# The tables of a state space layer: factors transposed once and read back, instead of a table transposed block by block

## The chip, the cores and the metric

The kernel runs on one core of a Trainium2 chip, as one launch. Its metric is device time in microseconds, the median of three runs. A profile of one further execution gives the busy time of each engine: TensorE (PE), VectorE (DVE), ScalarE (ACT), GpSimd (POOL) and SyncE (SP), which issues nearly all DMAs. All arithmetic is in float32; products on TensorE are made of exact parts (a value is split into a high part, `whi`, and a low part, `wlo`, and three products are added up).

## The reference

Two blocks follow each other on 256 tokens of 1024 features. The first has two layers, each with a mixer (pooling and a gated recurrence, then band attention), attention to a memory of 256 tokens, and an MLP with squared relu. The second has differential attention, an MLP, a state space layer and a last MLP. The state space layer is what the change is about:

```python
lam = lax.complex(a_re, a_im); dt = jnp.exp(log_dt)[..., None]
a_bar = jnp.exp(lam * dt)
b_bar = ((a_bar - 1.0) / lam)[..., None] * b_mat
def scan_dir(u_row, r, reverse):
    bu = jnp.einsum('sgh,gph->sgp', u_row.astype(jnp.complex64), b_bar[r])
    a = jnp.broadcast_to(a_bar[r], bu.shape)
    _, states = lax.associative_scan(_ssm_combine, (a, bu), reverse=reverse, axis=0)
    return jnp.einsum('sgp,ghp->sgh', states, c_mat[r]).real
```

There are 64 groups of 16 channels, each with 64 complex states in two directions. The kernel works through the scan in chunks of eight steps. For that it needs tables that depend on the weights alone: E, which carries eight inputs into the state at a chunk's end (powers of a times b), G, which reads eight outputs from the state at its start (powers of a times c), and the products of the two within a chunk.

## The kernel before, in words

The program is written layer by layer, and a scheduler orders the instructions of each engine by priority; each engine then runs its own list in order and waits on semaphores. Work that is marked `low` gets a lower priority, so that it falls between the instructions of the layer around it. DMAs on SP's queue are issued in order too, and a DMA that must wait for data holds up the ones behind it.

The four MLPs (`mlp`, line 275) have the same matmuls: for eight column chunks of 512, `ffps` is the product with the first weight, `relu` its squared relu, and `ffacc` adds up the product with the second. In the first two chunks the tokens are rows, and four `fftp` transposes turn each result (line 337); they come as matmuls with 512 columns. The other six chunks come as matmuls with 256. A weight tile of 512 KB is loaded (`raw`, line 42), its high part is made on ACT (lines 47 and 53) and its low part on DVE (lines 49 and 58).

An MLP can take a generator, `fill`, that it steps between its own products. The first MLP steps `ssm_scalars`: powers and phases of all 64 groups, on DVE, stored in `pk` and written to memory as `d_p`. The second MLP steps `ssm_tables` for blocks 0 to 7, the third for blocks 8 to 15 (a block has four groups); the fourth has no fill. The layer itself comes between the third and the fourth MLP and loads the tables again.

For a block, `ssm_tables` loads the coefficients (`bc`), the powers (`pk`) and the gain (`gb`). On DVE it makes `bb`, the input matrix, by a complex product. A complex product (`cmul`, line 1142) is four products and two combinations; with `second=G` two of its products run on GpSimd (lines 1149 and 1150). So come `er` and `gr`, with 512 columns for each real part. `gr` is written out as G. `er` has the states on the partitions and is turned by eight transposes into the `etp` tiles (line 1393); ACT copies them (`eo`, line 1394), and two DMAs write E (`d_e`). The klag matmuls (lines 1401 and 1405) make the products within a chunk from `bm` (copies of `bb`), the `c` part of `bc`, and `gr`.

Two pools matter on TensorE: `ps`, four PSUM banks that `ffps`, `fftp`, `etp` and `klag` share, and a second one of four banks for `ffacc`.

Of the kernel before, what the change touches and what calls it, by code (L numbers as in the profile page):

```python
# [24 lines left out]
class Seg:  # L25
    """A column block of a weight, its rows times a gain, split exactly into two float32r parts."""
# [42 lines left out]
class Core:  # L69
# [37 lines left out]
    def rstd(self, ms, n=1, scale=1.0, tag="r", bufs=None):  # L107
# [4 lines left out]
        if n >= 16:  # L112
            # a first guess from the exponent, then Newton's steps
# [19 lines left out]
    def feat_half(self, src, q, hi, lo, k0=None):  # L133
        """columns 512 q .. of src [128 tokens, 1024] -> hi, lo [128 features, 4 q .. (or k0 ..), 128 tokens]"""
# [15 lines left out]
    def row_scale_free(self, out):  # L150
        """the scales of the rows of X along the free axis: out [128, 256]"""
# [69 lines left out]
    def mm_b(self, out, wh, wl, xh, xl, first, last):  # L221
        """out [128 features, tokens] += w^T x"""
# [9 lines left out]
    def feat32(self, src, dst):  # L232
        """src [128 tokens, 1024] -> dst [128 features, 8, 128 tokens] in float32"""
# [8 lines left out]
    def proj_a(self, hh, hl, w, c0, done, gain=None, turns=((0, 0, 8), (1, 0, 8)), step=None, share=False, now=(0, 3)):  # L242
        """token-major [128, 1024] projections; the token tiles take turns: (tile, first and last step of the contraction)"""
# [15 lines left out]
    def proj_b(self, hh, hl, w, c0, consume, gain=None, groups=4):  # L259
        """feature-major projections of both token tiles: consume(g, [128 features, 2, 256]) for the columns 256 g .."""  # L260
# [14 lines left out]
    def mlp(self, pool, w1, gain, w2, done, perm=False, fill=None):  # L275
        """done(tt, acc, rsq): acc times rsq is the output; perm: tokens leave in the order (step in chunk, chunk)."""
# [116 lines left out]
class Halves:  # L393
    """activations [128, 2, 8, 128] in two tiles of four features each"""
# [9 lines left out]
class Attn:  # L404
    """attention sublayers; mixed into Core"""

    def mem_feat(self, parts, mem):
        """the memory over its root mean square, feature-major; kept for the other layer"""
# [23 lines left out]
    def two_parts(self, outs, src):  # L432
        """src as float32r parts"""
# [4 lines left out]
    def three(self, out, xs, ys, first, last):  # L438
        """out += x^T y, of float32r parts, or of float32 as it is"""
# [7 lines left out]
    def mem_keys(self, pool, parts, gain, w_kv, step=None):  # L447
        """feature-major: as float32r parts, or in float32 to take less room while there are steps to go along with"""
# [20 lines left out]
    def put_feat(self, ps, g, oh, ol):  # L469
        """ps [128 features, 2, 256 tokens] -> features 256 g .. as float32r parts"""  # L470
# [6 lines left out]
    def cross(self, pool, w_q, gain, kv, out, w_o, done):  # L477
        """out: the room for the heads' outputs, feature-major"""
# [56 lines left out]
    def band(self, pool, w_qkv, gain, relb, w_o, done):  # L535
        """relb: [16, 513]"""
# [10 lines left out]
        # the scales of the tokens along the free axis  # L547
# [8 lines left out]
        def scores(t, k0, nh):  # L556
            """heads of the features 128 k0 .. 128 (k0 + nh), queries of tile t"""
# [56 lines left out]
        def advance(g):  # L614
            """the scores of group g, the values of the group before"""
# [12 lines left out]
    def diff(self, pool, w_qkv, gain, q_gain, k_gain, lam_vecs, subln, w_o, cos2, sin2, done):  # L628
        """cos2, sin2: [256, 64], (cos | cos) and (-sin | sin)"""
# [32 lines left out]
        # the heads in two halves  # L662
# [11 lines left out]
        def part(c0, mid=None):  # L674
            """512 columns of both token tiles"""
# [12 lines left out]
        def prep(c, a, nm, dst):  # L688
            """rotated heads 8 c .. of both token tiles, feature-major; the root mean square is left to the scores for the queries"""
# [60 lines left out]
        def soft(t, g):  # L750
            """exponentials of the heads 4 g .. 4 g + 3; head 2 (2 g + i) + j is [j][i]"""
# [39 lines left out]
        def values(c):  # L791
            """the heads 4 c .. 4 c + 3, over their root mean square, into which the sums of the first softmax go"""
# [64 lines left out]
class Mixer:  # L857
    def even(self, pool, w_in, gain, pool_w, pool_scale, lb_logits, out_gain, w_out, masks, done, mem_feat, mem_keys):
        """pool_scale, lb_logits: [128, 4]; masks: [128, 5, 128]"""
# [90 lines left out]
        def queries(b, ps):  # L950
            """with the factor 1 - bound of the keys"""
# [6 lines left out]
        def pooling():  # L958
            """window sums by doubling, group g with the window 2 << g"""
# [19 lines left out]
        # decayed scores, transposed: [s, head, t] per token tile  # L979
# [27 lines left out]
        def levels():  # L1007
# [22 lines left out]
            # across the chunks of a tile, then across the tiles  # L1030
# [97 lines left out]
class Ssm:  # L1128
    """State space layer in chunks of L tokens. Groups are in the order (half, batch, q, strip) of group
    32 half + 8 strip + 4 batch + q; a block is four strips, a batch is four blocks."""  # L1130

    def ssm_scratch(self, dram):
# [3 lines left out]
        self.d_p = dram.tile([128, NG, 34], F32, name="d_p")  # L1136
# [5 lines left out]
    def cmul(self, pool, outr, outi, xr, xi, yr, yi, neg_i=False, tag="ct", second=None):  # L1142
        """(outr, outi) = x * y; with neg_i the imaginary part is negated"""
# [15 lines left out]
    def ssm_scalars(self, a_re, a_im, log_dt, sgn):  # L1159
# [700 lines left out]
```

## Time and profile before

| | |
|---|---|
| Median of three runs | 1508.09 us (1506.77 to 1510.31) |
| Span of the profiled execution | 1506.2 us |
| PE busy | 1426.7 us, 95% |
| DVE busy | 1138.3 us, 76% |
| ACT busy | 823.2 us, 55% |
| POOL busy | 203.4 us, 14% |
| DMA | 296.15 MB, mean 197 GB/s |

The profiled execution is known by its span, from the first to the last instruction; it lies 1.9 us below the median. The stages by time are: even mixer and memory attention to 231.8, first MLP to 416.0, band and memory attention to 641.1, second MLP to 863, differential attention to 989.2, third MLP to 1199.7, the state space layer to 1312, the last MLP to 1496. A busy share is a mean over these stages, and the limits differ between them, so a stage is read by itself: which engine is busy throughout, and what it waits for where it is not.

### The profile page before, as it was taken

To read this page: it belongs to the slowest core of one execution; us is meant where nothing else is said; L and a number is where in the kernel's file an instruction comes from. 1 tells how busy PE (TensorE), PEld (TensorE's weight loads), DVE (VectorE), ACT (ScalarE), POOL (GpSimd) and SP (SyncE) were. 2 spreads that over 40 slices of the span, in tenths; PEclk is the share of its full clock that TensorE was granted. 3 is DMA by queue.
4 is the path that set the end of the run, shared out by engine and by line. 5 is a ranking of instruction groups with operands and counts; after the bars stand their busy time and mean duration, and the time that the engine had idled before them with its cause. 6 is when DMAs were issued, how large, how long until landed. Compare 5 with 4: busy or idle time off the path is not lost.

```text
span 1506.2 us, 25237 instructions
## 1 busy us (share of the span) xinstructions
PE 1426.7 (95%) x9540; PEld 1239.2 (82%) x9540; DVE 1138.3 (76%) x2004; ACT 823.2 (55%) x1412; POOL 203.4 (14%) x219
## 2 busy tenths in 40 slices
PE   8899999999999999989899999999999877999997
PEld 8797888899889799869779877879789656889895
DVE  7986658988767775679994799889994688674651
ACT  7475546555564665655454777755453524664540
POOL 1241001000000000024430010124330131000000
PEclk9999999999999999999999999999999988999999
DMA  8455536465776355366667654256668956755640
GB/s 299 147 205 170 187 103 199 154 241 187 273 232 199 117 185 193 112 205 215 211 222 249 222 181 151 86 168 229 227 219 298 358 208 217 233 183 188 206 158 28
DMA packets 134034, 296.15 MB, mean 197 GB/s; under 512 B 16152, under 2 KB 36376, under 8 KB 133272
## 3 DMA queue, kind: packets, MB, share of 16 engines
q1 hardware_dynamic: 133624, 292.44, 57.8%
q0 software_dynamic: 288, 2.10, 0.4%
q8 instruction: 75, 1.23, 0.3%
q14 instruction: 47, 0.39, 0.1%
HBM read 269.10 MB, written 30.57 MB: 199 GB/s over the span
## 4 chain that ended last, share of the span: by engine, by line
PE 37%; DVE 15%; DMA 8%; issue 5%; ACT 2%; POOL 1%; SPq 0%; DVEq 0%; POOLq 0%; ACTq 0%
DVE wlo L58 4%; PE ffacc L218 4%; PE ffacc L219 4%; PE ffacc L217 4%; PE ffps L226 2%; PE ffps L224 2%; PE ffps L225 2%; DMA raw<-in_w_ff 2%; PE pacc L217 2%; PE pacc L218 2%; PE pacc L219 2%; DMA raw<-in_ffn_w_down 1%; DMA raw<-in_ffn_w_up 1%; PE pb L224 1%; PE pb L225 1%
## 5 line engine op out<-in xcount | busy, mean ns | idle before, releaser
L58 DVE SCALAR_TENSOR_TENSOR wlo<-raw,gcols,whi 128x512 fp32r<-128x512 f32 (+1 forms) x456 | 356.8, 825 | 68.8 <-ACT whi L53 68.5
L53 ACT ACTIVATE whi<-raw,gcols 128x512 fp32r<-128x512 f32 (+1 forms) x456 | 316.9, 745 | 126.5 <-DMA raw<-in_w_ff 26.9
L49 DVE TENSOR_TENSOR wlo<-raw,whi 128x1024 fp32r<-128x1024 f32 x172 | 207.1, 1221 | 64.9 <-ACT whi L47 64.4
L47 ACT ACTIVATE whi<-raw 128x1024 fp32r<-128x1024 f32 x176 | 182.1, 1055 | 91.7 <-DMA raw<-in_w_ff 28.3
L224 PE MATMUL ffps<-hh,whi 128*128 128x256 f32 x768 | 223.1, 290 | 0.0
L226 PE MATMUL ffps<-hl,whi 128*128 128x256 f32 x768 | 220.9, 288 | 0.0
L225 PE MATMUL ffps<-hh,wlo 128*128 128x256 f32 x768 | 220.5, 287 | 0.0
L217 PE MATMUL ffacc<-whi,ah 128*128 128x512 f32 x512 | 204.9, 401 | 0.0
L218 PE MATMUL ffacc<-wlo,ah 128*128 128x512 f32 x512 | 202.7, 396 | 0.1
L219 PE MATMUL ffacc<-whi,al 128*128 128x512 f32 x512 | 202.6, 396 | 0.0
L224 PEld LDWEIGHTS ffps<-hh,whi 128*128 128x128 f32 x768 | 149.3, 194 | 2.1 <-issue 1.6
L225 PEld LDWEIGHTS ffps<-hh,wlo 128*128 128x128 f32 x768 | 149.0, 194 | 0.5
L226 PEld LDWEIGHTS ffps<-hl,whi 128*128 128x128 f32 x768 | 148.8, 194 | 0.0
L219 PEld LDWEIGHTS ffacc<-whi,al 128*128 128x128 f32 x512 | 96.7, 189 | 22.9
L217 PEld LDWEIGHTS ffacc<-whi,ah 128*128 128x128 f32 x512 | 96.8, 189 | 22.5 <-issue 1.6
L218 PEld LDWEIGHTS ffacc<-wlo,ah 128*128 128x128 f32 x512 | 96.8, 189 | 21.5 <-DVE wlo L49 0.5
L225 PE MATMUL pb<-hh,wlo 128*128 128x256 f32 x352 | 100.5, 286 | 3.4 <-DVE wlo L58 3.4
L224 PE MATMUL pb<-hh,whi 128*128 128x256 f32 x352 | 100.1, 287 | 2.3 <-ACT whi L53 2.3
L226 PE MATMUL pb<-hl,whi 128*128 128x256 f32 x352 | 100.0, 285 | 0.0
L171 POOL TENSOR_TENSOR r<-r,mhalf 128x1 f32<-128x1 f32 x32 | 24.6, 768 | 535.0 <-DVE r L170 528.6
L299 DVE TENSOR_TENSOR relu<-relu 128x512 f32<-128x512 f32 x64 | 44.8, 701 | 59.1 <-ACT relu L298 58.9
L298 ACT ACTIVATE relu<-ffps 128x512 f32<-128x512 f32 x64 | 43.9, 686 | 76.9 <-PE ffps L226 62.7
(473 smaller groups left out, 3015.1 us busy)
## 6 DMA issues: line engine op xcount, KB each, us to landing
raw<-in_w_ff SPq DMA_DIRECT2D x128, 512.0 KB, 4.6
raw<-in_ffn_w_up SPq DMA_DIRECT2D x64, 512.0 KB, 4.4
raw<-in_ffn_w_down SPq DMA_DIRECT2D x64, 512.0 KB, 4.3
raw<-in_w_mem_kv SPq DMA_DIRECT2D x32, 512.0 KB, 4.6
raw<-in_w_qkv SPq DMA_DIRECT2D x24, 512.0 KB, 4.9
raw<-in_attn_w_qkv SPq DMA_DIRECT2D x24, 512.0 KB, 4.8
raw<-in_w_in_ab SPq DMA_DIRECT2D x20, 512.0 KB, 5.4
raw<-in_w_mem_q SPq DMA_DIRECT2D x16, 512.0 KB, 5.1
```

The source lines that it names most:

```text
L47: nc.scalar.activation(out=hi, in_=src, func=AF.Copy)
L49: eng.tensor_tensor(out=lo, in0=src, in1=hi.bitcast(F32), op=ALU.subtract)
L53: nc.scalar.activation(out=hi[:, a], in_=src[:, a], func=AF.Copy, scale=g)
L58: nc.vector.scalar_tensor_tensor(out=lo[:, a], in0=src[:, a], scalar=g, in1=hi[:, a].bitcast(F32), op0=ALU.mult, op1=ALU.subtract)
L217: nc.tensor.matmul(o, xh, wh[:, s], start=first, stop=False)
L218: nc.tensor.matmul(o, xh, wl[:, s], start=False, stop=False)
L219: nc.tensor.matmul(o, xl, wh[:, s], start=False, stop=last)
L224: nc.tensor.matmul(out, wh, xh, start=first, stop=False)
L225: nc.tensor.matmul(out, wl, xh, start=False, stop=False)
L226: nc.tensor.matmul(out, wh, xl, start=False, stop=last)
L298: nc.scalar.activation(out=o, in_=ps if view is None else ps.rearrange("p (f c j) -> p f c j", f=2, j=8), func=AF.Relu)
L299: nc.vector.tensor_tensor(out=r, in0=r, in1=r, op=ALU.mult)
```

## The change

Three things are made differently.

First, `ssm_scalars` makes both factors of E for all groups during the first MLP: the carry-out powers `pe`, eight for each of 64 groups, and the input matrices `bb`, in four steps of 16 groups, with their gain. `pe` is turned by eight TensorE transposes (tile `ptp`), `bb` by 16 (tile `btp`). ACT copies the results, which go to memory as `d_pt` and `d_bt`; `bb` itself goes there as `d_b`.

Second, a block of `ssm_tables` loads the turned factors repeated over the partitions: `pt` repeats each of eight rows 16 times, `bt` repeats 16 rows eight times, 512 KB each. Their complex product on DVE, two instructions of 1024 columns and two of 512, is E in its final layout and is written by one DMA. The per-block `bb` product, the `etp` transposes, the `eo` copies and the `er` products are gone.

Third, the G products are all on DVE.

```diff
+                pe = pool.tile([128, 16, 8, 4, 2], F32, name="pe")
...
-                self.cmul(pool, pk[:, :, 0:8], pk[:, :, 8:16], si[0], si[1], bw(w8r), bw(w8i))
-                nc.sync.dma_start(out=self.d_p, in_=pk)
+                po = [pe[:, :, :, :, ri].rearrange("p k j g -> p k g j") for ri in range(2)]
+                self.cmul(pool, *po, bk(si[0]), bk(si[1]), bk(bw(w8r)), bk(bw(w8i)))
+                nc.sync.dma_start(out=self.d_p, in_=pk[:, :, 0:16])
+                for h in range(2):
+                    tp = self.ps.tile([128, 4, 128], F32, tag="ps", name="ptp")
+                    for i in range(4):
+                        k0 = 8 * h + 2 * i
+                        nc.tensor.transpose(tp[:, i, :], pe[:, k0:k0 + 2].rearrange("p k j g r -> p (k j g r)"), self.ident)
+                    pt = pool.tile([128, 4, 128], F32, tag="pre_tp", name="pt")
+                    A.activation(out=pt, in_=tp, func=AF.Copy)
+                    nc.sync.dma_start(out=self.d_pt[512 * h:512 * h + 512].rearrange("(i p) n -> p i n", p=128), in_=pt)
             yield
+            for h in range(4):
+                gs = slice(16 * h, 16 * h + 16)
+                with self.low():
+                    bc = pool.tile([128, 16, 2, 16], F32, tag="pre_bc", name="bc")
+                    nc.sync.dma_start(out=bc, in_=bc4[:, gs, 0:2])
...
+                    V.tensor_tensor(out=bc, in0=bc, in1=gb.unsqueeze(2).to_broadcast([128, 16, 2, 16]), op=MU)
...
+                    self.cmul(pool, *bo, bk(bc[:, :, 0]), bk(bc[:, :, 1]), fb(16), fb(17), tag="ctb")
+                    nc.sync.dma_start(out=self.d_b[:, 4 * h:4 * h + 4], in_=bb)
+                    tp = self.ps.tile([128, 4, 128], F32, tag="ps", name="btp")
+                    for i in range(4):
+                        nc.tensor.transpose(tp[:, i, :], bb[:, i].rearrange("p c g r -> p (c g r)"), self.ident)
+                    bt = pool.tile([128, 4, 128], F32, tag="pre_tp", name="bt")
+                    A.activation(out=bt, in_=tp, func=AF.Copy)
+                    nc.sync.dma_start(out=self.d_bt[512 * h:512 * h + 512].rearrange("(i p) n -> p i n", p=128), in_=bt)
+                yield
...
             def first(k):
                 gs = slice(4 * k, 4 * k + 4)
                 with self.low(90):
-                    bc = pool.tile([128, 4, 4, 16], F32, tag="bc", name="bc", bufs=3)
-                    nc.sync.dma_start(out=bc, in_=bc4[:, gs])
...
+                    pt = pool.tile([128, 4, 2, 128], F32, tag="pt", name="pt", bufs=2)
+                    src = bass.AP(self.d_pt.tensor, self.d_pt.offset + k * 64 * 128, [[1024, 8], [0, 16], [1, 1024]])
+                    nc.sync.dma_start(out=pt.rearrange("p g r n -> p (g r n)"), in_=src)
+                    bt = pool.tile([128, 4, 2, 128], F32, tag="bt", name="bt", bufs=3)
+                    src = bass.AP(self.d_bt.tensor, self.d_bt.offset + k * 128 * 128, [[0, 8], [1024, 16], [1, 1024]])
+                    nc.sync.dma_start(out=bt.rearrange("p g r n -> p (g r n)"), in_=src)
+                    cc = pool.tile([128, 4, 2, 16], F32, tag="cc", name="cc", bufs=3)
+                    nc.sync.dma_start(out=cc, in_=bc4[:, gs, 2:4])
+                    pk = pool.tile([128, 4, 16], F32, tag="pk", name="pk", bufs=2)
                     nc.sync.dma_start(out=pk, in_=self.d_p[:, gs])
...
-                    self.cmul(pool, bb[:, 0], bb[:, 1], br, bi, fb(32), fb(33), tag="ctb")
-                    V.tensor_tensor(out=bb, in0=bb, in1=gb.unsqueeze(1).to_broadcast([128, 2, 4, 16]), op=MU)
+                    bb = pool.tile([128, 16, 4, 2], F32, tag="bb", name="bb", bufs=2)
+                    nc.sync.dma_start(out=bb, in_=self.d_b[:, k])
...
-                    er = pool.tile([128, 2, 4, 8, 16], F32, tag="er", name="er", bufs=2)
+                    et = pool.tile([128, 4, 2, 128], F32, tag="et", name="et")
+                    V.tensor_tensor(out=et, in0=bt[:, :, ::-1], in1=pt[:, :, 1:2].to_broadcast([128, 4, 2, 128]), op=MU)
+                    V.tensor_tensor(out=bt, in0=bt, in1=pt[:, :, 0:1].to_broadcast([128, 4, 2, 128]), op=MU)
+                    V.tensor_tensor(out=bt[:, :, 0], in0=bt[:, :, 0], in1=et[:, :, 0], op=SU)
+                    V.tensor_tensor(out=bt[:, :, 1], in0=bt[:, :, 1], in1=et[:, :, 1], op=AD)
+                    nc.sync.dma_start(out=self.d_e[k], in_=bt.rearrange("p g r n -> p (g r n)"))
...
-                    self.cmul(pool, er[:, 0], er[:, 1], pj(0), pj(8), vi(bb[:, 0]), vi(bb[:, 1]), tag="cte", second=G)
...
-                    self.cmul(pool, gr[:, :, 0], gr[:, :, 1], pj(16), pj(24), vi(cr), vi(ci), neg_i=True, tag="cte", second=G)
+                    self.cmul(pool, gr[:, :, 0], gr[:, :, 1], pj(0), pj(8), vi(cr), vi(ci), neg_i=True, tag="cte")
...
-                        for ri in range(2):
-                            nc.tensor.transpose(ps[:, 2 * j + ri, :], er[:, ri, 2 * g2 + j].rearrange("p a b -> p (a b)"), self.ident)
-                    A.activation(out=eo.rearrange("p g r n -> p (g r) n"), in_=ps, func=AF.Copy)
-                    nc.sync.dma_start(out=self.d_e[k, :, g2 * 512:g2 * 512 + 512], in_=eo.rearrange("p g r n -> p (g r n)"))
```

The order of the instructions moves with it. On TensorE, in the first MLP, the last of the four `fftp` groups before stands between the matmuls of chunk 2:

```order
L224 MATMUL ffps<-hh,whi 128x256
L225 MATMUL ffps<-hh,wlo 128x256
L226 MATMUL ffps<-hl,whi 128x256
L337 MATMUL fftp<-ident,relu 128x128 x4
L224 MATMUL ffps<-hh,whi 128x256
L225 MATMUL ffps<-hh,wlo 128x256
```

In the changed kernel all of chunk 2's matmuls, chunk 0's `ffacc` and half of chunk 1's come first, and then:

```order
L217 MATMUL ffacc_3018<-whi,ah 128x512
L218 MATMUL ffacc_3018<-wlo,ah 128x512
L219 MATMUL ffacc_3018<-whi,al 128x512
L1342 MATMUL ptp<-ident,pe 128x128 x5
L337 MATMUL fftp<-ident,relu 128x128 x4
L1364 MATMUL btp<-ident,bb 128x128 x4
L217 MATMUL ffacc_3019<-whi,ah 128x512
```

Five of the eight new `ptp` transposes, which read `pe`, and four `btp` stand around `fftp`, ahead of the second half of chunk 1's `ffacc`; the other three `ptp` and nine `btp` stand behind it, ahead of three chunks of `ffps`, and the last three `btp` among the last `ffacc` of the stage.

On DVE, in the same stage, the product that ends in `pk` stands before among weight splits (`wlo`) and the phases of the steps (`w5r`, `wr`, `tb`):

```order
L1185 SCALAR_TENSOR_TENSOR wi<-wi,wr 128x64
L58 SCALAR_TENSOR_TENSOR wlo<-raw,gcols,whi 128x512 x2
L1181 TENSOR_TENSOR wr<-sq_2841,sq_2842 128x64
L1296 COPY w5i_2848<-wi 128x64
L1151 TENSOR_TENSOR pk<-si,w8r 128x64x8
L1295 COPY w5r_2847<-wr 128x64
L1152 TENSOR_TENSOR pk<-si,w8i 128x64x8
L1149 TENSOR_TENSOR cmt<-si,w8i 128x512
L1150 TENSOR_TENSOR cmt_2928<-si,w8r 128x512
L1153 TENSOR_TENSOR pk<-pk,cmt 128x64x8
L1157 TENSOR_TENSOR pk<-pk,cmt_2928 128x64x8
```

In the changed kernel the product that ends in `pe` has the input factors `bb` of the first 16 groups beside it:

```order
L1189 SCALAR_TENSOR_TENSOR wi<-wi,wr 128x64
L1155 TENSOR_TENSOR pe<-si,w8i 128x16x4x8
L1185 TENSOR_TENSOR wr<-sq_2845,sq_2846 128x64
L1301 COPY w5i_2852<-wi 128x64
L1160 TENSOR_TENSOR bb<-bb,cmt_3001 128x4x4x16
L1300 COPY w5r_2851<-wr 128x64
L1152 TENSOR_TENSOR cmt<-si,w8i 128x512
L1153 TENSOR_TENSOR cmt_2932<-si,w8r 128x512
L1156 TENSOR_TENSOR pe<-pe,cmt 128x16x4x8
L1160 TENSOR_TENSOR pe<-pe,cmt_2932 128x16x4x8
```

The two weight splits between the steps are gone there: the whole chain of scalars stands earlier among the splits of the MLP than before.

On SP, early in the second MLP, before:

```order
L1752 DMA X<-d_x 128x1x1024 x2
L42 DMA raw<-in_w_ff 128x1024
L1358 DMA bc<-in_ssm_bc 128x256
L1360 DMA pk<-d_p 128x136
L1362 DMA gb<-in_ssm_g 128x64
L1358 DMA bc<-in_ssm_bc 128x256
L1383 DMA d_g<-gr 128x1024
L42 DMA raw<-in_w_ff 128x1024 x2
L1360 DMA pk<-d_p 128x136
L1362 DMA gb<-in_ssm_g 128x64
```

In the changed kernel, from the second block's loads on:

```order
L1398 DMA pt<-d_pt 128x1x1024
L1420 DMA d_e<-bt 128x1024
L1401 DMA bt<-d_bt 128x1x1024
L1403 DMA cc<-in_ssm_bc 128x4x32
L1405 DMA pk<-d_p 128x64
L1407 DMA bb<-d_b 128x128
L42 DMA raw<-in_w_ff 128x1024
L1429 DMA d_g<-gr 128x1024
L42 DMA raw<-in_w_ff 128x1024
L42 DMA raw<-in_w_ff 128x2x512 x2
```

A block's three loads (`bc`, `pk`, `gb`) became five (`pt`, `bt`, `cc`, `pk`, `bb`), and the store of E (`d_e`) stands ahead of the loads that come behind it in the queue.

## Rows read from the trace of the kernel before

**Rows 1.** Stretches: us; busy PE, PEld, DVE, ACT, POOL; granted clock; DMA share; GB/s.

```profile
core 0 of [0], span 1506.2 us
231.80:416.00 184.20, 184.20 (x1090) 162.50 (x1089) 157.53 (x421) 100.99 (x149) 7.41 (x18) 1.00 0.64 215
240.00:312.00 72.00, 72.00 (x453) 64.67 (x453) 66.31 (x213) 40.55 (x59) 0.38 (x1) 1.00 0.56 184
641.00:794.00 153.00, 137.63 (x1018) 119.24 (x1016) 140.06 (x226) 84.15 (x150) 54.41 (x47) 0.94 0.65 215
670.20:677.00 6.80, 4.73 (x23) 4.76 (x24) 6.36 (x16) 5.69 (x9) 1.77 (x2) 0.50 0.48 164
989.00:1131.00 142.00, 134.02 (x1005) 116.85 (x1006) 136.21 (x217) 74.28 (x142) 52.07 (x45) 0.96 0.63 214
```

**Rows 2.** TensorE's waits in 640:868: us in total, times, longest.

```profile
PE fftp L337 <- DVE relu L299: 5.7, 1, 5.7
PE etp L1393 <- ACT eo L1394: 5.1, 2, 3.0
```

**Rows 3.** DVE by line and shape, 231.8:416: busy us, mean ns, idle before.

```profile
L49 DVE TENSOR_TENSOR wlo<-raw,whi 128x1024 fp32r<-128x1024 f32 x32 | 38.5, 1221 | 6.1 <-ACT whi L47 6.0
L58 DVE SCALAR_TENSOR_TENSOR wlo<-raw,gcols,whi 128x512 fp32r<-128x512 f32 x51 | 35.5, 746 | 0.0
L1150 DVE TENSOR_TENSOR cmt<-tb,w5r 128x256 f32<-128x256 f32 x4 | 1.7, 424 | 0.0
```

**Rows 4.** Tile pk in 300:320: ns min/median/max, first and last start us.

```profile
L1157 DVE TENSOR_TENSOR pk<-pk,cmt x1: 689/689/689, 314.1 to 314.1; 128x512 f32<-128x512 f32 x1
```

**Rows 5.** DVE and GpSimd by line and shape, 641:794.

```profile
L58 DVE SCALAR_TENSOR_TENSOR wlo<-raw,gcols,whi 128x512 fp32r<-128x512 f32 x43 | 36.1, 882 | 1.8 <-ACT whi L53 1.8
L1149 POOL TENSOR_TENSOR cmt<-pk,bb 128x512 f32<-128x512 f32 x8 | 14.8, 1844 | 47.0 <-issue 39.6 <-DVE bb L1367 7.4
L1151 DVE TENSOR_TENSOR er<-pk,bb 128x512 f32<-128x512 f32 x8 | 8.9, 1117 | 0.0
L1153 DVE TENSOR_TENSOR gr<-gr,cmt 128x512 f32<-128x512 f32 x8 | 8.9, 1115 | 0.0
L1151 DVE TENSOR_TENSOR gr<-pk,bc 128x512 f32<-128x512 f32 x8 | 8.1, 1007 | 0.0
L1152 DVE TENSOR_TENSOR er<-pk,bb 128x512 f32<-128x512 f32 x8 | 7.2, 900 | 0.0
L1153 DVE TENSOR_TENSOR er<-er,cmt 128x512 f32<-128x512 f32 x8 | 7.2, 894 | 1.9 <-POOL cmt L1149 1.9
```

**Rows 6.** DVE by line and shape, 989:1131.

```profile
L58 DVE SCALAR_TENSOR_TENSOR wlo<-raw,gcols,whi 128x512 fp32r<-128x512 f32 x39 | 36.2, 972 | 2.5 <-ACT whi L53 2.5
L1153 DVE TENSOR_TENSOR gr<-gr,cmt 128x512 f32<-128x512 f32 x8 | 9.8, 1221 | 1.0 <-POOL cmt L1149 1.0
L1151 DVE TENSOR_TENSOR er<-pk,bb 128x512 f32<-128x512 f32 x8 | 8.7, 1093 | 0.0
```

**Rows 7.** Last step of the G tables, 640:868 and then 1000:1131.

```profile
L1155 DVE SCALAR_TENSOR_TENSOR gr<-gr,cmt x8: 677/678/682, 664.4 to 782.3; 128x512 f32<-128x512 f32 x8
...
L1155 DVE SCALAR_TENSOR_TENSOR gr<-gr,cmt x8: 677/679/684, 1003.7 to 1118.4; 128x512 f32<-128x512 f32 x8
```

**Rows 8.** Main DMA queue; X<-d_x: issue, first uses; tenths of DMA engines, 652:664.

```profile
q1 hardware_dynamic: 133624, 292.44, 57.8%
...
652.86 1.29 SPq L1752 DMA_DIRECT2D X<-d_x  x2
...
662.88 0.64 ACT L168 ACTIVATE junk<-X 128x512 f32<-128x512 f32 x1 [6.43 <-DMA X<-d_x]
667.86 0.63 ACT L168 ACTIVATE junk<-X 128x512 f32<-128x512 f32 x1 [1.18 <-DMA X<-d_x]
...
DMA  4679644602212396899998999999622222222222
```

More of the change, by code (lines that the diff above doesn't have):

```diff
@@ L1157, in cmul, with ssm_scalars @@
             V.tensor_tensor(out=outi, in0=outi, in1=t2, op=ALU.add)
-    def ssm_scalars(self, a_re, a_im, log_dt, sgn):
+    def ssm_scalars(self, a_re, a_im, log_dt, sgn, bc4, gain):
         nc, n = self.nc, NG
@@ new lines, in ssm_scalars @@
+            yield
+            for h in range(4):
[3 more added lines that the diff above has]
+                    nc.sync.dma_start(out=bc, in_=bc4[:, gs, 0:2])
+                    gb = pool.tile([128, 16, 16], F32, tag="pre_gb", name="gb")
+                    nc.sync.dma_start(out=gb, in_=gain[gs].partition_broadcast(128))
+                    V.tensor_tensor(out=bc, in0=bc, in1=gb.unsqueeze(2).to_broadcast([128, 16, 2, 16]), op=MU)
+                    bb = pool.tile([128, 4, 16, 4, 2], F32, tag="pre_bb", name="bb")
+                    bk = lambda ap: ap.rearrange("p (k g) c -> p k g c", g=4)
+                    bo = [bb[:, :, :, :, ri].rearrange("p k c g -> p k g c") for ri in range(2)]
+                    fb = lambda i: bk(pk[:, gs, i:i + 1].to_broadcast([128, 16, 16]))
+                    self.cmul(pool, *bo, bk(bc[:, :, 0]), bk(bc[:, :, 1]), fb(16), fb(17), tag="ctb")
[7 more added lines that the diff above has]
+                yield
@@ L1343, in ssm_scalars, with ssm_tables @@
                 yield
-    def ssm_tables(self, blocks, bc4, gain, d_rows, dmask):
+    def ssm_tables(self, blocks, bc4, d_rows, dmask):
         nc = self.nc
         V, A, G = nc.vector, nc.scalar, nc.gpsimd
-        MU, AD = ALU.mult, ALU.add
+        MU, AD, SU = ALU.mult, ALU.add, ALU.subtract
         F, B = FWD, BWD
@@ L1370, in first @@
                     G.memset(bm[B, :, :, 16:32], 0.0)
-                    A.activation(out=bm[:, :, :, 0:16], in_=bb, func=AF.Copy)
-                    A.activation(out=bm[F, :, :, 16:32], in_=bb[F], func=AF.Copy)
-                    A.activation(out=bm[B, :, :, 32:48], in_=bb[B], func=AF.Copy)
-                    er = pool.tile([128, 2, 4, 8, 16], F32, tag="er", name="er", bufs=2)
+                    b4 = bb.rearrange("p c g r -> p r g c")
+                    A.activation(out=bm[:, :, :, 0:16], in_=b4, func=AF.Copy)
@@ L1375, in first @@
+                    V.tensor_tensor(out=bt[:, :, 1], in0=bt[:, :, 1], in1=et[:, :, 1], op=AD)
+                    nc.sync.dma_start(out=self.d_e[k], in_=bt.rearrange("p g r n -> p (g r n)"))
+                yield
+                with self.low(90):
                     pj = lambda i: pk[:, :, i:i + 8].unsqueeze(3).to_broadcast([128, 4, 8, 16])
                     vi = lambda ap: ap.unsqueeze(2).to_broadcast([128, 4, 8, 16])
-                    self.cmul(pool, er[:, 0], er[:, 1], pj(0), pj(8), vi(bb[:, 0]), vi(bb[:, 1]), tag="cte", second=G)
@@ L1383, in first @@
                     nc.sync.dma_start(out=self.d_g[k], in_=gr.rearrange("p g r a b -> p (g r a b)"))
-                yield k, bc, bm, er, gr
-            def second(k, bc, bm, er, gr):
-                cr, ci = bc[:, :, 2], bc[:, :, 3]
-                for g2 in range(2):
-                    eo = pool.tile([128, 2, 2, 128], F32, tag="eo", name="eo", bufs=2)
-                    ps = self.ps.tile([128, 4, 128], F32, tag="ps", name="etp")
-                    for j in range(2):
-                        for ri in range(2):
-                            nc.tensor.transpose(ps[:, 2 * j + ri, :], er[:, ri, 2 * g2 + j].rearrange("p a b -> p (a b)"), self.ident)
-                    A.activation(out=eo.rearrange("p g r n -> p (g r) n"), in_=ps, func=AF.Copy)
-                    nc.sync.dma_start(out=self.d_e[k, :, g2 * 512:g2 * 512 + 512], in_=eo.rearrange("p g r n -> p (g r n)"))
-                    yield
+                yield k, cc, bm, gr
@@ L1397, in second @@
+            def second(k, cc, bm, gr):
+                yield
+                cr, ci = cc[:, :, 0], cc[:, :, 1]
                 ps = self.ps.tile([128, 144], F32, tag="ps", name="klag")
@@ L1743, in first_block @@
             c.mlp(pool, A["w_ff1"][l], gc[2], A["w_ff2"][l], lambda t, a, q: c.residual(t, a, post, q), perm=l == 1,
-                  fill=tables(c, A, range(8)) if l == 1 else c.ssm_scalars(A["ssm_a_re_2"], A["ssm_a_im_2"], A["ssm_log_dt_2"], c.sgn))
+                  fill=tables(c, A, range(8)) if l == 1 else c.ssm_scalars(A["ssm_a_re_2"], A["ssm_a_im_2"], A["ssm_log_dt_2"], c.sgn, A["ssm_bc"], A["ssm_g"]))
 def reorder(c):
@@ L1760, in tables @@
 def tables(c, A, blocks, last=False):
-    yield from c.ssm_tables(blocks, A["ssm_bc"], A["ssm_g"], c.d_rows, c.dmask)
+    yield from c.ssm_tables(blocks, A["ssm_bc"], c.d_rows, c.dmask)
     if last:
```

23 lines of the change are left out of this document (11 added, 12 removed).

## The prediction, made before the changed kernel was run

> **What bounds the kernel now.** I read the stages first, each engine's busy time in a stretch [rows 1]. In the first MLP stage, 231.8 to 416.0, TensorE is busy for all of its 184.2 us at full clock: matmuls alone set that stage, and all four MLP stages have the same matmuls. The second takes 221.9 us (641.1 to 863.0) and the third 210.5 (989.2 to 1199.7), so the tables made beside them cost some 37 and 26 us. Of that, 8 us each are extra TensorE work at the first stage's rate (below): 64 transposes of 128 columns, and in klag 64 matmuls of 128 columns and 64 of 16.
>
> Next, TensorE's waits. In the second MLP it waits 5.7 us for relu and 5.1 in two waits of etp, which are named for ACT but stand behind the table products [rows 2]. After a wait the granted clock is at its lower level, 1.2 instead of 2.4 GHz: 0.50 over 6.8 us behind the 5.7 us wait, which costs 3.4 us more [rows 1].
>
> Last, why the products are late. DVE is busy 140 of 153 us up to the last klag of the second MLP, and 136 of 142 in the third [rows 1], so the tables are bound by DVE. Part of that is GpSimd: beside its products of about 1.8 us, DVE instructions that take 0.68 us elsewhere have means of 0.9 to 1.12, and the 512-column weight split takes 0.88 instead of 0.746 [rows 3, 5].
>
> **The change, part by part.** *Factors, first MLP.* The carry-out powers (pe) and the input factors (bb) are made and transposed once, 24 transposes in all. That is 1.4 us at the stage's rate (one MLP is 393,216 columns of matmuls, 184.2 us, so 2.13 columns/ns), perhaps 3 with their start-up; I take 2. What matters more is where they stand. TensorE runs in order, and the changed order has five ptp transposes behind 96 + 72 matmuls of 512 columns, 96 of 256 and 12 transposes of the stage: 110,592 columns, 51.8 us, and 1 for the transposes. TensorE is there at 231.8 + 52.8 = 284.6 us. The transposes need both halves of pe from DVE.
>
> Before, the same pair of products, into pk, ended at 314.1 + 0.7 = 314.8 us [rows 4], and nothing on TensorE asked for them. In the changed order DVE has, ahead of this point, 8 fewer splits of 512 columns, 4 fewer of 1024 and 5 fewer of relu and al: 8 x 0.746 + 4 x 1.221 + 5 x 0.69 = 14.3 us [rows 3, 4]. It has 4 more products of 256 columns and one more of 512, 4 x 0.42 + 0.69 = 2.4. Instructions in a row overlap a little, so I take 11 us net: pe is there at 303.8. Before, DVE was busy for 66.3 of the 72 us from 240 to 312 [rows 1], so at most 5.7 us of idleness could be closed up. TensorE thus stands for 14 to 19 us; I take 19. Behind these transposes in its queue are fftp, ffacc and the ffps of three chunks, work that was ready.
>
> A second place: nine btp transposes in a row, 18 us of matmuls later, need the factors of the next groups, four times the gain product and six of 256 columns, which with the weights between are about 19.6 us on DVE. That is 323.4 against 321.8 on TensorE: 1 us. For the clock after so long a wait I take the 3.4 us above. Sum: 2 + 19 + 1 + 3 = **25 us lost** in the first MLP. Nothing hides it, since TensorE was never idle there. DVE has room to catch up: it is busy 157.5 of 184.2 us.
>
> *Tables, second and third MLP.* Gone are 128 transposes, their 32 evictions and the GpSimd products. A block now takes two DVE products of 1024 columns and two of 512 for E, and six of 512 for G. Before it was eight of 512 and eight small ones on DVE, four on GpSimd. By 1.22 and 0.68 us that is 7.9 against about 7.2 [rows 3, 5].
>
> TensorE's order is packed closer. The last klag stands about 95 us of matmuls into the stage instead of 124, and 95 us of the stage's work stand behind it instead of 67. If the tables never held TensorE up, a stage would take 184 us and klag's, 9,216 columns or 4 us and somewhat more for their start-up, 190 in all: 31 us gained in the second MLP, 20 in the third. But DVE's own work up to the last G table hardly shrinks. By the two orders and the durations of the rows it is 99.5 us before and 100.3 now, counted from the first relu; the added products cancel the fewer weight splits ahead. What is gained is the slowdown by GpSimd. For the second MLP: 43 x (0.882 - 0.746) = 5.8, and 8 x (0.44 + 0.22 + 0.21 + 0.44 + 0.33) = 13.1 for the er and gr products, 19 with rounding [rows 5]. For the third: 39 x 0.226 = 8.8, and 8 x (0.54 + 0.41 + 0.33) = 10.2, again 19 [rows 6] (the third product has the same mean in both stages [rows 5]). The last G table came at 783.0 and 1119.1 [rows 7]; it comes at 783 - 19 + 1 = 765 and at 1119 - 19 + 2 = 1102. With 95 us behind it, the stages end at 860 (-3) and 1197 (-2.5). TensorE is then idle for some 28 us ahead of the klags, where it was slower and fuller before.
>
> *The repeated reads.* Each block now loads pt and bt, 512 KB each, from sources whose outermost count is 8. The nearest row is X<-d_x, outermost count 4: two loads of 512 KB, issued at 652.9, of which the second landed 5.0 us after the first: ACT, which waits for them, starts at 662.88 and at 667.86. While they ran, the slices of 0.3 us up to 664 show 0.2 of the DMA engines busy, about four of 16 [rows 8]. 512 KB through four engines takes 5.0 us, so through eight 2.5, and a block puts 2 x 2.5 us on those eight that it did not before: 40 us for eight blocks. The engines were busy for 0.65 x 153 = 99 us up to the last klag of the second MLP, and 0.63 x 142 = 89 in the third [rows 1]. Nine weight loads less stand ahead; a load costs, at the page's 292.44 MB for 57.8% of 16 x 1506 us, 1.56 us on each engine [rows 8], so 14 us go. On the eight engines that makes 99 - 14 + 40 = 125 us and 115, against 124 and 113 us of DVE. So the transfers just reach DVE's bound: end at 641 + 125 + 95 = 861, and 989 + 115 + 95 = 1199. I take -2 and 0.
>
> The Trainium skill bears on this ("DMA: Bandwidth & Descriptors", "Rules for kernel authors"): an outermost dimension of fewer than 16 confines the whole transfer to at most as many engines, a leading zero-stride broadcast among its examples. The trace agrees for X<-d_x, at 5.0 us; if instead all 16 engines shared these loads, they would have 99 - 14 + 20 = 105 us of work and DVE alone would bound, the -3 and -2.5 above.
>
> **Sum.** 25 - 2 - 0 = +23 on the profiled execution. Its span is 1506.2 us [rows 1], and the three timed runs have a median of 1508.09, 1.9 above it, which I add unchanged: 1531. As the wait may close up by 5 us and the bound in the tables is drawn by a hair, I put the forecast at **1529 us**. The order of the other stages shifts too; I count that as nothing, give or take 4 us.
>
> **Rivals.**
> *The factors come in time* (faster). The order is fixed, but if DVE reaches pe by about 290, the first MLP loses only some 7 us, and the tables' gains, 5.5 by DVE's bound, more if DVE also closes its 13 idle us of the second stage, win: 1508 + 7 - 18 = 1497. Against it: DVE was 92% busy up to this point.
> *TensorE is hardly held in the tables* (faster). The early reads of the next blocks and the even pace of DVE let the closer packing pay: four fifths of 31 + 20, or 40, against the 25 lost: 1508 + 25 - 40 = 1493. For it: every transposition and eviction is gone from the chain. Against it: DVE's 100 us against 95 of TensorE's, in the order itself.
> *Eight engines are overfull* (slower, and more than forecast). Weight loads queue behind 16 long reads on the same engines; at 90% of what the engines can do the 125 and 115 us become 139 and 128, so +14 and +13 on those two stages: 1529 + 2 + 25 = 1556 at worst, 1540 halfway.
>
> **How the numbers follow.** Forecast 0.52, its own range 1517 to 1537; overfull engines 0.20; factors in time 0.14; TensorE free 0.14. The first two are slower, 0.72; of the two faster ones I leave 0.03 for no change, that is within 0.2% (3 us), about what a measurement of this kernel can tell from none, and 0.25 for faster. For 8 times in 10 I leave out a tenth at each end: 1494 to 1546.
>
> **What would show it.** Right: one TensorE wait of 14 to 20 us at ptp near 285 us, released by DVE's pe, and half clock behind it; DVE products at 0.68 us throughout, 512-column splits at 0.75; waits of TensorE at klag in both table stages, behind DVE's G products or behind loads of pt and bt, whose landing takes over 4 us. Wrong: a first MLP within 8 us of 184; a second MLP under 205 us; DVE waiting long for bt, with weight loads landing in over 8 us, which would be the third rival.

## The result, and the profile after

The changed kernel takes 1609.59 us (median of four runs, 1603.53 to 1611.07) against 1509.2 for the kernel before on the same chip: a ratio of 1.066, 95% interval 1.0643 to 1.0679. I forecast slower, 1529, and gave a range up to 1546: the direction was right, the size a fifth of what came. The profiled execution has a span of 1601.7 us, 95.5 above that of before. By stages, from the start of an MLP's first ffps matmul to the start of its last ffacc matmul:

| us | before | forecast | after |
|---|---|---|---|
| first MLP (factors made and transposed) | 183.8 | +25 | 224.6 (+40.8) |
| second MLP (tables 0 to 7) | 221.3 | -2 | 247.7 (+26.4) |
| third MLP (tables 8 to 15) | 210.1 | 0 | 235.4 (+25.3) |
| fourth MLP | 183.0 | 0 | 182.9 |
| all between them | | 0 | +3.1 |

TensorE's waits in the first MLP, changed kernel (total us, times, longest):

```profile
PE ptp L1342 <- DVE pe L1160: 19.8, 1, 19.8
PE btp L1364 <- DVE cmt L1153: 8.3, 1, 8.3
PE btp L1364 <- DVE bb L1160: 4.7, 1, 4.7
```

The first is the wait that I forecast. The two at btp are 13 us where I had 1. Before, there was none in this stage. While TensorE stands at btp, DVE's longest idle time (5.9 us) is for a load, and the clock is low behind each wait:

```profile
DVE bc L1355 <- DMA bc<-in_ssm_bc: 8.3, 3, 5.9
...
232.90:457.50 224.60, 191.61 (x1112) 168.19 (x1111) 171.38 (x448) 104.15 (x154) 7.59 (x18) 0.92 0.60 186
300.00:310.00 10.00, 4.33 (x17) 3.81 (x18) 7.72 (x20) 3.19 (x6) 0.00 (x0) 0.50 0.64 85
330.00:340.00 10.00, 1.09 (x4) 0.72 (x4) 4.05 (x9) 1.19 (x2) 0.00 (x0) 0.57 0.78 213
```

(The lower rows are stretches, columns as in [rows 1]; the granted clock is the number before the DMA share.) So the 40.8 us are 33.0 of standing and 7.8 of longer busy time, 191.6 us where it was 183.8: the 24 transposes, and matmuls at the lower clock.

In the table stages, up to the last klag, the stretches that answer to those of [rows 1] are:

```profile
685.00:838.00 153.00, 119.98 (x822) 98.98 (x823) 111.03 (x163) 64.40 (x115) 4.80 (x15) 0.85 0.74 227
1061.00:1192.00 131.00, 114.69 (x828) 96.15 (x826) 106.35 (x155) 57.09 (x107) 3.33 (x13) 0.92 0.80 247
```

DVE is now busy for 111 us of 153, not 140, and TensorE for 120, not 138: neither bounds the stage any more. Behind the last klag the second MLP takes the 95 us of the forecast, 838 to 933; the loss lies ahead of it. What is waited for instead, DVE first and then ACT, 685 to 838:

```profile
DVE et L1416 <- DMA bt<-d_bt: 23.3, 5, 9.2
...
ACT bm L1412 <- DMA bb<-d_b: 30.3, 7, 5.9
ACT junk L168 <- DMA X<-d_x: 10.6, 1, 10.6
ACT whi L47 <- DMA raw<-in_w_ff: 9.1, 4, 4.2
```

So the bound has moved to transfers, although all DMA engines together are busy for only 0.74 of the stretch. DVE's own instructions are as forecast; against [rows 5] the slowed ones are back at 0.69 and 0.747 us:

```profile
L58 DVE SCALAR_TENSOR_TENSOR wlo<-raw,gcols,whi 128x512 fp32r<-128x512 f32 x31 | 21.7, 747 | 7.4 <-ACT whi L53 7.4
...
L1416 DVE TENSOR_TENSOR et<-bt,pt 128x1024 f32<-128x1024 f32 x8 | 9.8, 1225 | 23.3 <-DMA bt<-d_bt 23.3
...
L1156 DVE TENSOR_TENSOR gr<-gr,cmt 128x512 f32<-128x512 f32 x8 | 5.5, 689 | 0.0
```

### The profile page after: what moved, and what is told of

The parts are those of the page before. It is cut to its first block, busy times and chain, and to the rows that moved or that the text cites. A ratio compares the mean times of both kernels' runs of the same rounds, so it can differ in the third digit from the quotient of the medians.

```text
span 1601.7 us, 24821 instructions
## 1 busy us (share of the span) xinstructions
PE 1444.8 (90%) x9436; PEld 1245.8 (78%) x9436; DVE 1127.5 (70%) x1952; ACT 821.0 (51%) x1386; POOL 107.5 (7%) x155
## 4 chain that ended last, share of the span: by engine, by line
PE 40%; DVE 11%; DMA 10%; issue 3%; ACT 2%; SPq 1%; POOL 1%; DVEq 0%; ACTq 0%; POOLq 0%
PE ffacc L217 4%; PE ffacc L218 4%; PE ffacc L219 4%; PE ffps L225 3%; PE ffps L226 3%; PE ffps L224 3%; DMA bt<-d_bt 3%; DMA bb<-d_b 2%; DVE wlo L58 2%; PE pacc L217 2%; PE pacc L219 2%; PE pacc L218 2%; DMA raw<-in_ffn_w_down 1%; DMA raw<-in_w_ff 1%; PE pb L224 1%
## 5 line engine op out<-in xcount | busy, mean ns | idle before, releaser
L58 DVE SCALAR_TENSOR_TENSOR wlo<-raw,gcols,whi 128x512 fp32r<-128x512 f32 (+1 forms) x456 | 342.1, 794 | 70.9 <-ACT whi L53 70.7
L218 PE MATMUL ffacc<-wlo,ah 128*128 128x512 f32 x512 | 206.8, 404 | 1.7 <-DVE wlo L49 1.7
L219 PEld LDWEIGHTS ffacc<-whi,al 128*128 128x128 f32 x512 | 98.8, 193 | 23.3
```

The costliest lines, as they stand in the source:

```text
L58: nc.vector.scalar_tensor_tensor(out=lo[:, a], in0=src[:, a], scalar=g, in1=hi[:, a].bitcast(F32), op0=ALU.mult, op1=ALU.subtract)
L218: nc.tensor.matmul(o, xh, wl[:, s], start=False, stop=False)
L219: nc.tensor.matmul(o, xl, wh[:, s], start=False, stop=last)
```

## The experiments

Runs without an interval are one execution each, read by its stages; the fourth MLP, which none of them touches, is 182.9 or 183.0 us in all.

**e1, transposes late.** All 24 transposes stand behind 24 empty steps of the generator.

```diff
-                        nc.tensor.transpose(tp[:, i, :], pe[:, k0:k0 + 2]...   (and those of bb)
+            for _ in range(24):
+                yield
+            (the same transposes and copies here)
```

> The changed kernel with the 24 factor transposes of the first MLP moved to about 392 us on TensorE's list (24 empty steps of the generator ahead of them, the input factors kept in four tiles); all else as changed. Theory A (TensorE stands for factors that DVE has not made): the first MLP takes 185 to 190 us instead of 224.6, the other stages stay within 3 us, the kernel comes to about 1570. Rival B (DVE itself falls behind by the added products and their loads, whatever TensorE's order): the first MLP still takes over 205 us, with waits of TensorE for weight splits.

Measured: first MLP 221.3, a time of 1604.5. Up to 371 us TensorE does not wait at all, so the old waits are gone, but new ones took their place:

```profile
PE btp L1386 <- ACT pt L1378: 17.3, 2, 14.0
PE ffacc L218 <- DVE wlo L49: 3.8, 2, 3.3
```

The six copies share one staging tile, and each waits until the store of the one before has landed (ACT waits 14.0 us for d_pt, of which the first 7.5 go by before SP, held up by weight loads, issues that store). Theory A is neither shown nor refuted by the time; its forecast of 185 to 190 fell. The over 205 us of rival B came, but for the most part from the staging tile, as e7 shows.

**e7, the same with six staging tiles.**

```diff
-                    pt = pool.tile([128, 4, 128], F32, tag="pre_tp", name="pt")
+                    pt = pool.tile([128, 4, 128], F32, tag=("pre_tp", "pre_si0")[h], name="pt")     (and four more tags for bt)
```

> The late transposes of e1 with six staging tiles for their copies instead of one, so that no copy waits for the store of the one before. Theory E (what was left of the loss in the first MLP of e1 was the round trip copy, store, copy through one tile, 17.3 us of waits and the half clock behind them): the first MLP takes 195 to 203 us instead of 221.3. Rival: the stores and loads of the first MLP themselves are in the way, and the stage stays over 212.

Measured: first MLP 201.2, as theory E had it, a time of 1585.0. So of the 40.8 us, 23.4 go with the transposes' place and the single tile together. The rest, 17.4, is some 11 us in which TensorE stands and some 6.5 by which it is busy longer than before (last row), with the 24 transposes and the lower clock behind the waits. Three waits make 9.1 of the 11; why the two for a weight (whi, wlo) come is open:

```profile
PE ffacc L218 <- DVE wlo L49: 3.3, 1, 3.3
PE btp L1386 <- ACT pt L1378: 3.0, 1, 3.0
PE ffacc L217 <- ACT whi L47: 2.8, 1, 2.8
...
232.00:433.40 201.40, 190.41 (x1112) 166.12 (x1111) 172.69 (x449) 105.19 (x156) 5.03 (x16) 0.98 0.69 208
```

**e2, a quarter of the repeated reads.**

```diff
-                    src = bass.AP(..., [[1024, 8], [0, 16], [1, 1024]])
+                    src = bass.AP(..., [[1024, 8], [0, 16], [1, 256]])     (bt likewise)
```

> The changed kernel with a quarter of the repeated reads: pt and bt are loaded with 256 columns instead of 1024 and the products read them four times over, with the same DVE work and the same number of DMAs; three quarters of the factors are left out of E. Theory C (the repeated reads on eight DMA engines set the table stages): the second and third MLP take some 210 and 198 us instead of 247.7 and 235.4, waits of DVE for bt go. Rival D (the queue: loads stand behind stores that wait for DVE, a block's chain is serial): both stages stay above 235 and 225 us.

Measured: second and third MLP 217.5 and 211.1, 30.2 and 24.3 less; DVE's wait for bt is 0.8 us and ACT's for bb 4.8:

```profile
DVE et L1417 <- DMA b<-d_bt: 0.8, 1, 0.8
...
ACT bm L1413 <- DMA bb<-d_b: 4.8, 2, 4.4
...
688.70:813.10 124.40, 112.84 (x829) 93.67 (x827) 110.53 (x161) 66.28 (x117) 5.18 (x15) 0.95 0.69 233
```

Theory C holds in kind, though both stages are slower than the 210 and 198 that it named; D falls. With cheap reads the tables are about back at the time of before (221.3, 210.1), no more.

**e8, a quarter of bt alone.**

> The changed kernel with a quarter of bt's bytes alone (256 of 1024 columns, read four times over by the products), pt whole; three quarters of the input factors are left out of E. In the trace of the changed kernel packets of pt take 160 ns and packets of bt, whose eight engines read the same rows at a time, some 250. If that is the cost, bt alone gives back 60% of the 30 and 24 us that a quarter of both gave: 230 and 221 us. If only bytes count, half: 233 and 223, hardly to be told from it. If it is bt's place in the chain (DVE waits for bt, never for pt): nearly all of it, 220 and 213.

Measured: 225.6 and 219.1, that is 73% and 67% of e2's gain. That bt costs more than pt is not shown by this: no run cuts pt alone, and the first quarter taken away may simply bring more than the second. Nor is it settled which load has the packets of 250 ns: in a stretch with such packets, 797 to 801 us (shown with e12), the load at work is by SP's order of issue pt.

**e5 and e6, other queues.** The stores, and then the two loads, on GpSimd's queue.

```diff
-                    nc.sync.dma_start(out=self.d_e[k], ...)        (e5; d_g and d_kl too)
+                    nc.gpsimd.dma_start(out=self.d_e[k], ...)
-                    nc.sync.dma_start(out=pt..., in_=src)          (e6; bt too)
+                    nc.gpsimd.dma_start(out=pt..., in_=src)
```

> The changed kernel with the stores of E, G and the products within a chunk (d_e, d_g, d_kl) issued from GpSimd's queue, which is empty here, instead of SP's, where they held the queue up while they waited for DVE. Theory D (SP's queue sets the table stages): second and third MLP shrink from 247.7 and 235.4 us to under 230 and 220. Theory C (eight DMA engines busy with the repeated reads): they stay within 8 us, since the bytes and the engines are the same, and waits for pt and bt stay.

> The changed kernel with the two repeated loads (pt, bt) issued from GpSimd's queue instead of SP's; bytes and shapes are the same. Theory C, if such loads sit on the same eight engines whoever issues them: the table stages stay within 8 us of 247.7 and 235.4. If GpSimd's queue spreads them over other engines, packets in flight rise from 8 towards 16 and the stages shrink towards 217 and 211, those of the run with a quarter of the bytes. Theory D would have it in between, since SP's other loads no longer stand behind these.

Measured: e5 251.9 and 250.7, e6 251.4 and 241.9: no gain in either, and a loss in the third MLP of e5. Up to the last klag of the second MLP, the wait of DVE for bt did shrink, to 5.8 us in e5 and to none in e6, but ACT then waited 46 us for weights in each, where the changed kernel has 13.5. The rows are e5's:

```profile
DVE et L1416 <- DMA bt<-d_bt: 5.8, 1, 5.8
...
ACT whi L53 <- DMA raw<-in_w_ff: 32.1, 13, 7.3
ACT whi L47 <- DMA raw<-in_w_ff: 13.9, 4, 6.2
```

So the wait moved to other loads and did not go. The gain of theory D did not come: the order of SP's queue alone is not what held the tables up. If GpSimd's queue put the loads of e6 on other engines, it brought nothing.

**e9, four engines.** Each load as two DMAs of 64 partitions.

```diff
+                    for q in range(2):
+                        src = bass.AP(..., [[1024, 4], [0, 16], [1, 1024]])
```

> The changed kernel with each repeated load cut into two DMAs of 64 partitions, whose outermost count is 4 instead of 8: the same bytes on half as many engines, two more issues a block. Theory C1 (the few engines are the limit): four packets at a time in these loads, 10 us and more for a pair on four engines where it was 6.6 on eight, and the table stages 25 to 50 us longer each than 247.7 and 235.4. Theory C2 (only the bytes, or the rows read again and again, cost): within 8 us of them.

Measured: 290.5 and 286.3, +43 and +51. The same bytes on half the engines, and up to the last klag all engines together are busy for a smaller share of the time, while DVE waits longer:

```profile
687.50:882.70 195.20, 125.23 (x828) 102.23 (x826) 112.20 (x163) 66.64 (x117) 5.69 (x15) 0.79 0.56 181
...
DVE et L1418 <- DMA bt<-d_bt: 31.5, 6, 11.9
```

The direction is theory C1's. The size is not the engines' alone: the two more DMAs a block changed the order on every queue, and SP, by the sum of its issues up to the last klag, took 85.7 us to issue 109 DMAs, where the changed kernel took 47.0 for 93.

**e3, sixteen engines in pieces.** Eight DMAs of 16 partitions for each load.

> The changed kernel with each of the two repeated loads cut into eight DMAs of 16 partitions and 64 KB, whose outermost count is 16; the bytes are the same. Theory C1 (eight engines are too few): 16 packets at a time instead of eight, packets of 4096 bytes near 200 ns, the table stages 15 to 30 us shorter each. Theory C2 (the same rows, read 8 or 16 times over, are slow whichever engine reads them): packets still take near 300 ns in such loads and the stages stay within 8 us. Rival D (SP's queue): 14 more issues a block make the stages longer, by up to 8 x 14 x 0.4 = 45 us each.

Measured: 302.3 and 293.4, 55 and 58 longer than with one DMA for each load. This told nothing of the engines: the scheduler cut the pieces in among other DMAs, SP issued 204 DMAs up to the last klag instead of 93, and the issues took it 86.9 us instead of 47.0. Rival D had up to 45 us for that. SP also waited 37 us for E's product and 29 for G's, ahead of pieces that DVE then needed, but in the changed kernel it waited 34 and 19 for the same. So theory D, by the issues rather than by the waits, is a likely cause of this kernel's time, not a shown one.

**e12, sixteen engines by the order of rows.** The one experiment in which the instructions stand in the same order on every engine: the bytes are the same, and what moves is the number of DMA engines and, with it, the order in which the rows are read.

```diff
-[[1024, 8], [0, 16], [1, 1024]]      -[[0, 8], [1024, 16], [1, 1024]]
+[[0, 16], [1024, 8], [1, 1024]]      +[[1024, 16], [0, 8], [1, 1024]]
```

> The changed kernel with the two repeated loads read in the other order of rows: pt with a leading count of 16 repeats, then 8 rows; bt with 16 rows, then 8 repeats. Both now lead with 16 instead of 8; bytes, DMAs, and the order on every engine are the same instruction for instruction. E comes out with its rows in another order (channel before step), which the layer then reads as if it were not so. Theory C1 (eight engines are the limit): second and third MLP fall from 247.7 and 235.4 us towards 217 and 211, the run with a quarter of the bytes; I expect 215 to 228 and 208 to 220, and some 45 us in all, 1560. Theory C2 (what costs is reading the same rows again and again, or the 16 MB): they stay within 8 us. Theory D (the queue's order, which is unchanged): the same.

Measured: 233.3 and 218.4, 14.4 and 17.0 less; a ratio to before of 1.045 (1.0428 to 1.0471) where the changed kernel has 1.066. The time is 1577 where I had 1560. The engines now are busy for more of the stretch, and DVE waits for bt less than half as long:

```profile
684.40:822.40 138.00, 116.44 (x828) 96.40 (x826) 111.36 (x163) 64.75 (x115) 4.80 (x15) 0.90 0.84 255
...
DVE et L1416 <- DMA bt<-d_bt: 10.4, 4, 4.7
```

The number of engines can be read from the DMA share (the last number but one) while the engines are at these loads: half of the 16 in the changed kernel, all of them in e12, and a quarter for X<-d_x in the kernel before, whose count is 4:

```profile
797.00:801.00 4.00, 2.00 (x10) 2.00 (x11) 3.81 (x5) 1.19 (x3) 0.00 (x0) 0.50 0.52 132
801.00:802.50 1.50, 1.50 (x9) 1.50 (x8) 1.50 (x4) 0.00 (x0) 0.00 (x0) 0.50 0.52 205
...
781.00:783.00 2.00, 2.00 (x19) 2.00 (x18) 0.11 (x1) 0.00 (x0) 0.00 (x0) 1.00 1.02 238
...
662.00:665.00 3.00, 3.00 (x14) 2.45 (x13) 0.74 (x3) 2.12 (x6) 0.45 (x1) 1.00 0.26 105
```

Theory C1 is right in kind. I expected up to 228 and 220, and the second MLP stayed above that: the number of engines is 31 of the 54.5 us that e2 gave back. The other 23 go with the bytes, at 0.84 of all engines, as far as e2, in which the order of instructions moved too, can tell.

The Trainium skill has this as a rule ("DMA: Bandwidth & Descriptors", "Rules for kernel authors"): an outermost dimension of fewer than 16 keeps the whole DMA on at most that many engines, and one whose size is a multiple of 16 should stand there. The runs agree: 8 and 16 in that place, with all else in the same order, give 247.7 and 233.3 us. With 4, and another order, it is 290.5 (e9), and e3's 302.3, which has 16 there in smaller DMAs, shows that the rule is not all that counts.

**e10 and e13, both mended.**

> e7 (late transposes, six copies) and e2 (a quarter of the repeated reads, three quarters of the factors left out of E) in one. If the two causes are separate, their gains add up: first MLP 201, second 217, third 211, a time of 1585 - 30 - 25 = 1530, still 20 slower than before. If they hang together (the queues that the first fills spill into the second), it comes to under 1520.

> e7 (late transposes, six copies) with the loads of e12, E's rows in the other order again. If the two causes account for the loss: first MLP 201, second and third as in e12, a time of e12's less 23 us, 1530 to 1540, still some 25 slower than before; what then stays is 17 us in the first MLP and tables that gain nothing. If eight engines are not the limit, 1580 as in e7.

Measured: e10 1525.2, with 200.6, 219.3 and 212.1, so the two causes add up to within 5 us of the time that I gave; e13 1552.1, above the 1530 to 1540, with 201.5, 239.8 and 215.8. e13's second MLP is 6 us longer than e12's, and e1's and e7's are 6 and 4 longer than the changed kernel's, though the DMAs of that stage stand in the same order. The four times of the changed kernel span 7.5 us, so it may be no more than that; I have no cause. Even e10, which leaves most of the reads out, is not faster than before.

**e4 and e11, the third part alone.** The kernel before, with its products on DVE.

```diff
-self.cmul(pool, er[:, 0], er[:, 1], pj(0), pj(8), vi(bb[:, 0]), vi(bb[:, 1]), tag="cte", second=G)
+self.cmul(pool, er[:, 0], er[:, 1], pj(0), pj(8), vi(bb[:, 0]), vi(bb[:, 1]), tag="cte")     (gr too)
```

> The kernel before with its four GpSimd products a block on DVE instead: the third part of the change alone. By the prediction's term DVE loses the slowdown (19 us a stage) and gains 32 products of 0.6 us (19 us): second and third MLP stay within 5 us of 221 and 210, weight splits of 512 columns are at 0.75 us. Rival: GpSimd's products cost nothing but time on paper, so DVE's added 19 us make the stages 15 to 20 us longer.

> The kernel of e4 again, timed: the kernel before with its table products on DVE alone. One run gave 1494.5 beside 1513 of before; the trace's stages say 11 us in the second MLP and none in the third. I expect a median of 1493 to 1498 and a ratio to before of 0.988 to 0.993, faster beyond the interval. Rival: the single run was lucky, ratio 0.997 to 1.0.

Measured: second MLP 210.0 (-11.3), third 210.4; timed, 1500.18 against 1509.25, ratio 0.9937 (0.9919 to 0.9956): faster than both kernels, if by a little less than the 0.988 to 0.993 that I gave. My forecast of no change in the second MLP fell. DVE does 22 us more of products there (four groups of eight at 0.69) and is busy for less than before [rows 1]:

```profile
641.00:780.20 139.20, 131.82 (x1015) 114.49 (x1016) 129.64 (x247) 82.17 (x147) 5.16 (x15) 0.98 0.67 221
...
PE ffps L224 <- ACT whi L53: 11.0, 1, 11.0
ACT whi L53 <- DMA raw<-in_ffn_w_up: 27.2, 8, 19.8
```

The second row is TensorE's one wait in the third MLP: the waits at etp are gone, and 11.0 us for a weight have come in their place, where ACT waits up to 19.8 us for `raw` (third row). So the third stage's gain was taken back; why that load came so late no run shows.

## Why the prediction was right in direction and wrong in size

*Bounds before.* Right: the tables were bound by DVE, and GpSimd slowed it (e4). The size was low. I had 19 us of slowdown; in e11 DVE is busy 10.4 us less up to the last klag with 22 us more of products. Some 8 of that are weight splits that stand behind the last klag there (six of 512 columns, three of 1024), so the slowdown was nearer 24. One count was half: the trace has 128 klag matmuls of 128 columns and 128 of 16 in a stage, where I had 64 of each. It is TensorE's work, which did not bound these stages.

*TensorE stands at ptp.* Right: 19 forecast, 19.8 measured, released by DVE's pe. TensorE stopped at 285.9 us (forecast 284.6) and pe was there at 305.6 (forecast 303.8), so each side was read to within 2 us, and the two errors nearly cancel. It was read from the order of two engines and one row of the trace.

*The second place, btp: 1 us.* This step failed: 13.0 us. I summed DVE's instructions and left out what they wait for. From pe to the factors that the ninth btp needs I had 19.6 us; it took 36, in which DVE stood for 13.7, 8.3 of them for bc. The longest of these waits shows the chain, in order of time:

```profile
333.07 0.60 ACT L1366 ACTIVATE bt<-btp 128x512 f32<-128x512 f32 x1 [3.76 <-DMA d_pt<-pt]
333.69 0.38 SPq L1367 DMA_DIRECT2D d_bt<-bt  x1
334.12 0.56 SPq L1352 DMA_DIRECT2D bc<-in_ssm_bc  x1
338.46 0.69 DVE L1355 TENSOR_TENSOR bc<-bc,gb 128x512 f32<-128x512 f32 x1 [5.91 <-DMA bc<-in_ssm_bc]
```

ACT's copy waited for the one staging tile (Theory E's, 20 us from e1 to e7, where the transposes stood together), the store of bt for the copy, and the load of bc stood behind that store on SP. bc has one buffer, which was free at 331.6 us, so the queue cost 2.5 us here, and the rest is that no earlier load was possible. This is read from the trace; no run changes bc's buffers or its place. The clock cost more too: TensorE ran 9.0 us at 0.50 behind the three waits, which costs some 4.5 where I had 3.4.

*The repeated reads: -2 and 0.* This step failed, and it is most of the miss: +26 and +25. The kind was right, the loads do sit on eight engines (e12), and I named it as a rival, overfull engines, with 1540 to 1556; the size was not. I took 2.5 us for 512 KB on eight engines, from X<-d_x running alone, summed 125 us, and set them beside DVE's 124 as if the larger of the two would count. The stretch took 153. The 2.5 us are too few at least at times: from 797 to 801 half of the engines carried 132 GB/s, or 4.0 us for 512 KB (205 GB/s, or 2.6 us, just behind). Three more things were left out, as I read it. The sum holds only if these eight engines never idle. If each weight and each small load (bb, cc, pk) has a share on the same eight, it lands when the slowest of them is through: ACT waited 30.3 us for bb, 64 KB a time, and 13.3 in e12. And DVE's work stood behind the loads, not beside them: it waited 23.3 us for bt. How the loss divides among these is not shown. What the engines cost is 31 us by e12, and the bytes some 23 more by e2.

*No gain in the tables even then.* Forecast -3 and -2.5 by DVE's bound; e2 measured -3.8 and +1.0, and its last klag ended 124.4 us into the second MLP, where I had the last G table at 124. That part of the working stands, in part by luck, since it took the slowdown by GpSimd 5 us too low.

*Other stages.* +3.1 us, within the 4 that I gave.

The rivals in which the kernel came out faster were each wrong for the reason given against them: pe came at 305.6 us and not at 290, and even with cheap reads (e2) the closer packing gained nothing.

## What to carry to other kernels

Count a transfer by the engines that it runs on, not by the share of all: a source read with a repeat should lead with 16, and swapping the two outer dimensions can do that at no cost in bytes or instructions. The rows then come in another order, which whatever reads them must follow; e12's layer does not. When work is moved to be done once, look at where it stands in the in-order list of the busiest engine, and follow its inputs back through loads and single buffers, not only through the engine that makes them. Try the parts of a change alone: here the one that took work away from GpSimd gave 0.6% alone, and with the other two the kernel lost 6.6%.

## What was not expected of the hardware

The same loads from GpSimd's queue (e6) were no faster. In e9 the DMA engines' mean share fell from 0.74 to 0.56 while the stage grew by 43 us: a low share of all engines can hide a few that are full. In e9, too, SP took up to 4.8 us to issue one DMA, where 2.3 is the longest of the changed kernel's in this stretch. Open: why two weights come late in the first MLP of e7 (6 us), and the 6 us of e13.
